# Hybrid decoder layer on one core: low parts of the second branch's weight chunks by ScalarE and an adding DMA instead of a VectorE difference

## The chip, the cores and the metric

The kernel runs on one core of a Trainium2 chip. The metric is the device time of one execution in microseconds. A core has TensorE (matmuls; PE in the profile, PEld its weight loads), VectorE (DVE), ScalarE (ACT), GpSimd (POOL) and SyncE (SP), each with its own queue of instructions that it works off in order, and 16 DMA engines that these queues feed. Here SP's queue issues the plain loads and POOL's queue issues the DMAs that add onto their destination.

## The reference

One decoder layer on 512 tokens of width 1024, in float32. What matters here is its middle part:

```python
h = rms_norm(x, mix_norm)
(fq, fk, fv, ff, dq, dk, dv, iq, ik, iw, ga, gb) = split_columns(h @ w_in)
o_a = fox_attention(fq, fk, fv, log_f).reshape(B, S, FOX_W)               # 512 columns
o_b = dsa_attention(dq, dk, dv, iq, ik, iw, rel_bias).reshape(B, S, DSA_W) # 512 columns
merged = jax.nn.sigmoid(ga) * (o_a @ w_branch_a) + jax.nn.sigmoid(gb) * (o_b @ w_branch_b)
x = x + merged @ w_out
```

Before it and behind it stands a half-step feed-forward part, `x = x + 0.5 * swiglu_ffn(x, ...)`. The change touches how the weights `w_branch_b` (512 x 1024) are got ready.

## The kernel before

**Numbers in two parts.** Every large product is done in three matmuls of a faster 32-bit format (fp32r). A float32 operand is split into a high part, which is the value rounded to fp32r, and a low part, which is the value less the high part. `mm3` (L147 to L150) multiplies high by high, high by low and low by high into the same PSUM bank. Its three lines are the three matmul lines of the profile: for a weight chunk as the first operand, L148 and L149 read the chunk's high part `wh` and L150 its low part `wl`.

**A weight chunk.** `load_w` (L127 to L145) fetches one chunk: a DMA on SP's queue brings it into a raw tile (L136), ScalarE rounds it into `wh` (L137), and then `wl` is made. Without `adding`, VectorE subtracts `wh` from the raw tile (L143). With `adding`, ScalarE writes minus `wh` into `wl` (L140), and a DMA on POOL's queue adds the raw tile onto it (L141). Raw tiles go round over three tags `ra`, `rb`, `rc` with one buffer each; `wh` and `wl` have three buffers each. So a raw tile is free for the next load when its last reader is through (the subtraction, or the adding DMA), and chunk number n + 3 can be rounded only when the matmuls of chunk n have read `wh`. Chunks 6 to 15 of the projections (the set `ADDING`, L34) already take the adding path, and so do parts of the feed-forward stages (L122, L222, L241).

**The stage of the change.** It follows the attention. In order of the program it does:

- the last gate's product (`gb7`, L1317, 24 matmuls into `ps_gb`),
- eight sigmoids of gate A (`sa`, L1313 called at L1322) with a multiplication each on VectorE (L1323),
- a loop over eight blocks d of 128 output columns (L1324 to L1336): one chunk of `w_bb` with 128 x 512 numbers, 12 matmuls of 512 columns into a bank `ps_bb`, the sigmoid of gate B, two VectorE steps into `m` (L1331, L1332), and the split of `m` into `mh` on ScalarE (L1335) and `ml` on VectorE (L1336),
- a loop over eight blocks for `w_out` (L1337 to L1344): chunks of 128 x 1024 numbers by `load_w` without `adding`, 24 matmuls each into `ps_out`, of which the last three read `mh[7]` and `ml[7]`, an addition onto x and what the next norm needs.

The chunks of `w_bb` are called bb0 to bb7 below, those of `w_out` out0 to out7. Their raw tags follow one another as ra (bb0), rb (bb1), rc (bb2), ra (bb3), and so on to rb (bb7), rc (out0).

**What sets the order.** TensorE runs in the order of the program, written out by hand (L59). The order on ScalarE, VectorE, POOL and SP in this stage is made by a planner when the kernel is built: of the instructions that its own model has ready it takes the one that stands first in the program. The instructions of `load_w` count as 30 places earlier than they stand (`high_priority`, L135), and the sigmoids are kept behind the last copy of the attention's output (L1312). On the chip each engine then keeps that order, and waits at an instruction until its inputs and its buffer are there.

Of the kernel before, what the change touches and what calls it, by code (L numbers as in the profile page):

```python
# [19 lines left out]
P = 128  # L20
# [34 lines left out]
def tile_hybrid_layer(ctx: ExitStack, tc: tile.TileContext, a: dict):  # L55
# [11 lines left out]
    def acc_tile(name):  # L67
        return psum.tile([P, T], F32, tag="acc", bufs=3, name=name)

    def tmp_tile(name):  # L70
        return tmp.tile([P, T], F32, tag="t", name=name)
# [39 lines left out]
    def raw_tile(tag):  # L111
        return wpool.tile([P, 1024], F32, tag=tag, bufs=1, name=tag)
# [14 lines left out]
    def load_w(src, n, m, raw=None, adding=False):  # L127
        f = n * m
        if raw is None:
            raw = raw_tile(next(raw_tags))  # L130
        wh = wpool.tile([P, 1088], F32R, tag="wh", name="wh")
        wl = wpool.tile([P, 1088], F32R, tag="wl", name="wl")

        wh, wl = (w[:, at:at + f] for w in (wh, wl) for at in [8 if m > P else 0])
        with tc.high_priority(offset=1 if first else 30):  # L135
            nc.sync.dma_start(raw[:, :f].rearrange("p (n m) -> p n m", n=n), src)  # L136
            S.copy(wh, raw[:, :f])  # L137
            if adding:

                S.mul(wl, wh.bitcast(F32), -1.0)  # L140
                G.dma_start(wl, raw[:, :f], accum_op=OP.add)  # L141
            else:
                V.tensor_sub(wl, raw[:, :f], wh.bitcast(F32))  # L143
        return (wh.rearrange("p (n m) -> p n m", n=n),
                wl.rearrange("p (n m) -> p n m", n=n))  # L145

    def mm3(out, lh, ll, rh, rl, start, stop, **more):  # L147
        PE.matmul(out, lh, rh, start=start, stop=False, **more)  # L148
        PE.matmul(out, lh, rl, start=False, stop=False, **more)  # L149
        PE.matmul(out, ll, rh, start=False, stop=stop, **more)  # L150

    def prep(d, gi):

        g = gains[:, gi, d:d + 1]
        if d % 2 == 0:
            for i, (part, nm) in enumerate(((xh, "xh"), (xl, "xl"))):
                t = stream(HK * i + d // 2, F32R, nm)
                part[d], part[d + 1] = t[:, :T], t[:, T:]
        S.mul(xh[d], x[d], g)
        V.scalar_tensor_tensor(xl[d], x[d], g, xh[d].bitcast(F32), op0=OP.mult, op1=OP.subtract)  # L160
# [7 lines left out]
    def add_square(d, sq=None):  # L168
        sq = sq or square(d)
        if d == 0:  # L170
            ssq[0] = sq
        else:
            V.tensor_add(ssq[0], ssq[0], sq)
# [18 lines left out]
    def fm_product(w, name, midway={}, ps=None):  # L192
        ps = acc_tile(name) if ps is None else ps
        for k in range(KD):
            mm3(ps, w[0][:, k], w[1][:, k], xh[k], xl[k], k == 0, k == KD - 1)
            if k in midway:
                midway[k]()
        return ps
# [584 lines left out]
    with (tc.tile_pool(name="mix", bufs=1) as mp, ExitStack() as att_ctx,  # L783
# [523 lines left out]
        with tc.tile_pool(name="late", bufs=1) as lp:  # L1307
            mh, ml = [], []

            def sigmoid(out, z):  # L1310

                with tc.issue_after(last_out[0].ins):  # L1312
                    S.activation(out, z, AF.Sigmoid)  # L1313

            gb[6] = lp.tile([P, T], F32, name="gb6")
            nc.sync.dma_start(gb[6], kept[:, 4])
            ps = fm_product(load_w(a["w_gb"][7], KD, P), "ps_gb")  # L1317
            gb.append(lp.tile([P, T], F32, name="gb7"))
            V.tensor_mul(gb[7], ps, rb)
            for d in range(KD):  # L1320
                sa = lp.tile([P, T], F32, tag="sa", bufs=2, name="sa")
                sigmoid(sa, ga[d])  # L1322
                V.tensor_mul(pA[d], pA[d], sa)  # L1323
            for d in range(KD):  # L1324
                wh, wl = load_w(a["w_bb"][d], 4, P)
                ps = acc_tile("ps_bb")
                for k in range(4):
                    mm3(ps, wh[:, k], wl[:, k], oB[0][k], oB[1][k], k == 0, k == 3)
                sigmoid(gb[d], gb[d])
                m = tmp_tile("m")  # L1330
                V.tensor_mul(m, ps, gb[d])  # L1331
                V.tensor_add(m, m, pA[d])  # L1332
                mh.append(lp.tile([P, T], F32R, name=f"mh{d}"))
                ml.append(lp.tile([P, T], F32R, name=f"ml{d}"))
                S.copy(mh[d], m)  # L1335
                V.tensor_sub(ml[d], m, mh[d].bitcast(F32))  # L1336
            for d in range(KD):  # L1337
                wh, wl = load_w(a["w_out"][d], KD, P)
                ps = acc_tile("ps_out")
                for k in range(KD):  # L1340
                    mm3(ps, wh[:, k], wl[:, k], mh[k], ml[k], k == 0, k == KD - 1)
                V.tensor_add(x[d], ps, x[d])
                prep(d, 2)
                add_square(d)  # L1344
# [84 lines left out]
```

## Time and profile before

| What | Value |
|---|---|
| median of 3 runs | 1073.92 us (1073.33 to 1073.96) |
| profiled execution, its own time | 1073.57 us |
| profiled execution, its span from first to last instruction | 1071.9 us |
| TensorE busy | 1056.8 us, 99% of the span |
| VectorE, ScalarE, GpSimd busy | 78%, 62%, 23% |
| granted TensorE clock, mean | 0.998 |
| the eight `w_bb` products on TensorE | from 667.4 to 690.0 us of the span |

All rows of the profile are taken from the profiled execution, in microseconds from the start of its span. A row of the timeline gives start, duration, engine, line, operation and what is written from what; a bracket at its end gives how long the engine was idle before it and what ended that wait. Rows of TensorE overlap, since matmuls are pipelined: the distance of their starts is what one costs. A row of the DMA view gives the issue, its size and the time from the issue to the landing.

### The profile page before, as it was taken

To read this page: it belongs to the slowest core of one execution; us is meant where nothing else is said; L and a number is where in the kernel's file an instruction comes from. 1 tells how busy PE (TensorE), PEld (TensorE's weight loads), DVE (VectorE), ACT (ScalarE), POOL (GpSimd) and SP (SyncE) were. 2 spreads that over 40 slices of the span, in tenths; PEclk is the share of its full clock that TensorE was granted. 3 is DMA by queue.
4 is the path that set the end of the run, shared out by engine and by line. 5 is a ranking of instruction groups with operands and counts; after the bars stand their busy time and mean duration, and the time that the engine had idled before them with its cause. 6 is when DMAs were issued, how large, how long until landed. Compare 5 with 4: busy or idle time off the path is not lost.

```text
span 1071.9 us, 19227 instructions
## 1 busy us (share of the span) xinstructions
PE 1056.8 (99%) x7330; PEld 976.2 (91%) x7330; DVE 835.2 (78%) x1374; ACT 662.4 (62%) x1098; POOL 245.1 (23%) x313
## 2 busy tenths in 40 slices
PE   9999999999999999999999999999999999999998
PEld 7889999999998889999878788788889999999998
DVE  6987888897867579976776675954977788887887
ACT  6736765765664675477766756544635764775673
POOL 1100111120000014367786563000100210111111
PEclk9999999999999999999999999999999999999999
DMA  7644764666442267733313321442653665567554
GB/s 246 148 147 115 155 161 126 141 164 167 107 110 95 75 147 190 199 96 98 90 60 99 118 89 50 144 139 76 133 157 99 137 155 163 127 160 183 128 124 129
DMA packets 55677, 140.56 MB, mean 131 GB/s; under 512 B 6424, under 2 KB 14488, under 8 KB 55584
## 3 DMA queue, kind: packets, MB, share of 16 engines
q1 hardware_dynamic: 39888, 110.22, 33.8%
q0 software_dynamic: 15552, 28.84, 15.3%
q8 instruction: 58, 0.95, 0.4%
q10 hardware_dynamic: 144, 0.26, 0.1%
q14 instruction: 35, 0.29, 0.1%
HBM read 104.94 MB, written 3.42 MB: 101 GB/s over the span
## 4 chain that ended last, share of the span: by engine, by line
PE 79%; issue 7%; DVE 5%; ACT 4%; POOL 3%; DMA 1%; SPq 0%; DVEq 0%; POOLq 0%; ACTq 0%
PE pB L149 4%; PE pB L148 4%; PE pB L150 4%; PE pA L149 3%; PE pA L148 3%; PE ps_f L148 3%; PE pA L150 3%; PE ps_f L149 3%; PE ps_f L150 3%; PE dB L148 2%; PE dB L150 2%; PE dB L149 2%; PE ps_t L148 2%; PE ps_t L150 2%; PE ps_t L149 2%
## 5 line engine op out<-in xcount | busy, mean ns | idle before, releaser
L117 ACT CAST wh<-s 128x1024 fp32r<-128x1024 f32 (+1 forms) x84 | 81.8, 974 | 62.2 <-PE pC L149 31.1
L124 DVE TENSOR_TENSOR wl<-s,wh 128x1024 fp32r<-128x1024 f32 (+1 forms) x84 | 94.5, 1125 | 27.1 <-ACT wh L117 27.1
L148 PE MATMUL ps_t<-wh,xh 128*128 128x256 f32 (+1 forms) x288 | 80.7, 280 | 0.0
L150 PE MATMUL pB<-tbh,wl 128*128 128x256 f32 x288 | 80.4, 279 | 0.0
L148 PE MATMUL pB<-tbh,wh 128*128 128x256 f32 x288 | 80.4, 279 | 0.0
L149 PE MATMUL pB<-tbl,wh 128*128 128x256 f32 x288 | 80.4, 279 | 0.0
L149 PE MATMUL ps_t<-wl,xh 128*128 128x256 f32 (+1 forms) x288 | 80.3, 279 | 0.0
L150 PE MATMUL ps_t<-wh,xl 128*128 128x256 f32 (+1 forms) x288 | 80.2, 279 | 0.0
L148 PE MATMUL ps_f<-xh,wh 128*128 128x512 f32 x152 | 61.2, 403 | 0.0
L149 PE MATMUL ps_f<-xl,wh 128*128 128x512 f32 x152 | 60.3, 397 | 0.0
L150 PE MATMUL ps_f<-xh,wl 128*128 128x512 f32 x152 | 60.2, 396 | 0.0
L148 PEld LDWEIGHTS ps_t<-wh,xh 128*128 128x128 f32 x288 | 54.3, 188 | 0.5
L149 PEld LDWEIGHTS ps_t<-wl,xh 128*128 128x128 f32 x288 | 54.3, 188 | 0.5
L150 PEld LDWEIGHTS ps_t<-wh,xl 128*128 128x128 f32 x288 | 54.3, 188 | 0.0
L148 PEld LDWEIGHTS pB<-tbh,wh 128*128 128x128 f32 x288 | 54.1, 188 | 0.0
L150 PEld LDWEIGHTS pB<-tbh,wl 128*128 128x128 f32 x288 | 54.1, 188 | 0.0
L149 PEld LDWEIGHTS pB<-tbl,wh 128*128 128x128 f32 x288 | 54.1, 188 | 0.0
L241 POOL DMA_DIRECT2D b<-gu x10 | 8.7, 865 | 198.2 <-DVE rf L441 100.7
L1140 ACT ACTIVATE p<-p,mn 128x512 f32<-128x512 f32 (+1 forms) x64 | 36.0, 562 | 28.1 <-DVE mn L1138 27.6
L1142 POOL TENSOR_SCALAR p<-p,rs 128x512 f32<-128x512 f32 (+1 forms) x64 | 38.7, 607 | 60.1 <-DVE rs L1141 58.1
L1154 DVE TENSOR_TENSOR pl<-pt,ph 128x512 fp32r<-128x512 f32 (+1 forms) x64 | 31.1, 487 | 20.6 <-ACT ph L1153 19.9
L567 POOL DMA_DIRECT2D xa<-e x16 | 19.1, 1193 | 111.6 <-ACT wh L117 87.3
(398 smaller groups left out, 4144.6 us busy)
## 6 DMA issues: line engine op xcount, KB each, us to landing
ra<-in_w_pair_dram SPq DMA_DIRECT2D x15, 512.0 KB, 4.1
rc<-in_w_pair_dram SPq DMA_DIRECT2D x15, 512.0 KB, 4.0
re<-in_w_pair_dram SPq DMA_DIRECT2D x12, 512.0 KB, 3.6
rf<-in_w_pair_dram SPq DMA_DIRECT2D x12, 512.0 KB, 3.6
rb<-in_w_pair_dram SPq DMA_DIRECT2D x12, 512.0 KB, 3.6
xa<-e POOLq DMA_DIRECT2D x18, 256.0 KB, 3.7
rd<-in_w_halves_dram SPq DMA_DIRECT2D x10, 384.0 KB, 3.8
al<-gu POOLq DMA_DIRECT2D x14, 256.0 KB, 5.3
```

Source lines behind the costliest of these rows:

```text
L117: S.copy(wh[:, :f], raw[:, :f])
L124: V.tensor_sub(wl[:, :f], raw[:, :f], wh[:, :f].bitcast(F32))
L148: PE.matmul(out, lh, rh, start=start, stop=False, **more)
L149: PE.matmul(out, lh, rl, start=False, stop=False, **more)
L150: PE.matmul(out, ll, rh, start=False, stop=stop, **more)
L241: G.dma_start(l, src, accum_op=OP.add)
L567: G.dma_start(xa[:, d:d + 2, HT:], t["e"][part], accum_op=OP.add)
L1140: S.activation(p, p, AF.Exp, bias=mn, scale=-1.0, accum_out=rs)
L1142: G.tensor_scalar(p, p, rs, 1.0, op0=OP.mult, op1=OP.mult)
L1154: V.tensor_sub(pl[:, sl], pt[:, sl], ph[:, sl].bitcast(F32))
```

## The change

The eight chunks of `w_bb` are fetched with `adding=True`. `load_w` itself is as it was; the flag chooses the branch of L140 and L141 in place of L143.

```diff
             for d in range(KD):
-                wh, wl = load_w(a["w_bb"][d], 4, P)
+                wh, wl = load_w(a["w_bb"][d], 4, P, adding=True)
                 ps = acc_tile("ps_bb")
                 for k in range(4):
                     mm3(ps, wh[:, k], wl[:, k], oB[0][k], oB[1][k], k == 0, k == 3)
```

So in each of the eight steps a VectorE subtraction of 128 x 512 numbers goes, and a ScalarE multiplication by -1 of 128 x 512 numbers and a DMA of 256 KB on POOL's queue, which adds the raw tile onto `wl`, come in its place.

## The prediction

> **What bounds the kernel now.** I read the page's busy shares first, then the stage by windows, then the timelines of TensorE, ScalarE, VectorE and SP there, then the DMA view.
>
> ```profile
> PE 1056.8 (99%) x7330; PEld 976.2 (91%) x7330; DVE 835.2 (78%) x1374; ACT 662.4 (62%) x1098; POOL 245.1 (23%) x313
> ...
> 667.20:678.00 10.80, 10.37 (x46) 8.24 (x45) 8.62 (x16) 9.90 (x19) 0.00 (x0) 1.00 0.16 49
> 678.00:690.00 12.00, 12.00 (x55) 9.94 (x54) 12.00 (x21) 6.18 (x10) 0.00 (x0) 1.00 0.63 176
> 690.00:700.00 10.00, 9.07 (x40) 7.07 (x39) 8.57 (x12) 4.47 (x6) 0.00 (x0) 1.00 0.63 234
> ```
>
> TensorE is busy 99% of the span. The window rows give the length of a stretch and then the busy time of PE, PEld, DVE, ACT and POOL, the clock, the DMA share and GB/s. In the stage of the change (667 to 690 us) VectorE is packed full from 678 on, POOL does nothing at all, and the DMA engines are quiet up to 678. Yet TensorE loses only 0.43 and 0.93 us there. Its timeline shows where:
>
> ```profile
> 672.64 0.39 PE L150 MATMUL ps_bb<-oB,wl 128*128 128x512 f32 x1
> 672.87 0.39 PE L148 MATMUL ps_bb<-oB,wh 128*128 128x512 f32 x1
> 673.10 0.39 PE L149 MATMUL ps_bb<-oB,wh 128*128 128x512 f32 x1
> 673.92 0.50 PE L150 MATMUL ps_bb<-oB,wl 128*128 128x512 f32 x1 [0.43 <-DVE wl L143]
> ...
> 689.96 0.39 PE L148 MATMUL ps_out<-mh,wh 128*128 128x512 f32 x1
> ...
> 694.04 0.39 PE L148 MATMUL ps_out<-mh,wh 128*128 128x512 f32 x1
> 695.35 0.50 PE L149 MATMUL ps_out<-ml,wh 128*128 128x512 f32 x1 [0.93 <-DVE ml L1336]
> ```
>
> A matmul costs 0.23 us (672.64 to 672.87), so a chunk of 12 takes 2.72 us. The first wait is for the low part of bb2: its third matmul starts at 673.92 where 673.33 was due, 0.59 late. The second is for the last `ml`: 695.35 where 694.27 was due, 1.08 late. These 1.7 us are all that a lighter VectorE can give back. TensorE has no other wait from 667 to 700 that VectorE causes.
>
> **What goes.** Eight subtractions of the size of this one leave VectorE (0.68 us each, 0.60 from start to start):
>
> ```profile
> 673.18 0.69 DVE L143 TENSOR_TENSOR wl<-rc,wh 128x512 fp32r<-128x512 f32 x1
> ```
>
> That is 8 x 0.60 = 4.8 us of VectorE in a stage where it is full, enough to remove the 1.08 us at the end: gain 1.1 us. The 0.59 us is counted below, since its wait changes owner.
>
> **What comes, for one chunk.** The adding path is in the trace for other chunks. Here are two of the projections (128 x 1024), and one of the feed-forward part with the 128 x 512 size, by ScalarE, POOL and SP timeline, and by the DMA view (last rows; the landings of all adds into that tile, and the median of four of them in a stretch):
>
> ```profile
> 399.61 1.05 ACT L137 CAST wh<-ra 128x1024 fp32r<-128x1024 f32 x1 [2.74 <-PE ps_t L150]
> 400.70 1.06 ACT L140 ACTIVATE wl<-wh 128x1024 fp32r<-128x1024 f32 x1
> 405.21 1.05 ACT L137 CAST wh<-rb 128x1024 fp32r<-128x1024 f32 x1 [1.30 <-PE ps_t L150]
> 406.89 1.05 ACT L140 ACTIVATE wl<-wh 128x1024 fp32r<-128x1024 f32 x1
> ...
> 402.06 0.88 POOL L141 DMA_DIRECT2D wl<-ra  x1 [1.82 <-ACT wl L140]
> ...
> 407.96 0.33 SPq L136 DMA_DIRECT2D ra<-in_w_ga_dram  x1
> ...
> 299.60 0.64 ACT L221 ACTIVATE al<-ah 128x512 fp32r<-128x512 f32 x1
> ...
> DMA to landing us min/median/max: 3.3/4.6/5.8
> ...
> al<-gu POOLq DMA_DIRECT2D x4, 256.0 KB, 4.3
> ```
>
> The multiplication follows the cast at once (400.70, the cast ends 400.66) or lets another instruction in (406.89, 0.63 after the cast's end). POOL's issue starts 0.30 after the multiplication ends (400.70 + 1.06 = 401.76, issue 402.06). The raw tile is reloaded only when the add has landed: 407.96 is 5.9 us behind the issue at 402.06. For 256 KB a landing took 3.3 to 5.8 us from the issue, and those bounds I keep. I take 4.3, since the DMA share of 0.16 from 667 to 678 is a quiet stretch. So from the start of a cast the low part takes 0.62 (cast) + 0.04 + 0.64 + 0.30 + 4.3 = 5.9 us, or 6.4 with one other ScalarE instruction (0.52 from start to start) let in; the bounds are 4.9 and 7.9. By VectorE it was there at the end of the subtraction, 673.86, which is 2.2 us behind its cast.
>
> **Which chunks that reaches.** ScalarE's order in the stage, with TensorE's change from the gate product to bb0 and POOL's last work before it:
>
> ```profile
> 653.17 0.62 ACT L137 CAST wh<-ra 128x512 fp32r<-128x512 f32 x1
> 661.72 0.62 ACT L137 CAST wh<-rb 128x512 fp32r<-128x512 f32 x1 [0.45 <-PE ps_f L149]
> 666.99 3.22 ACT L1313 ACTIVATE gb<-gb 128x512 f32<-128x512 f32 x6
> 671.68 0.61 ACT L137 CAST wh<-rc 128x512 fp32r<-128x512 f32 x1
> 672.19 0.63 ACT L1313 ACTIVATE gb<-gb 128x512 f32<-128x512 f32 x1
> 672.72 0.60 ACT L137 CAST wh<-ra 128x512 fp32r<-128x512 f32 x1
> 674.79 0.62 ACT L137 CAST wh<-rb 128x512 fp32r<-128x512 f32 x1
> ...
> 667.20 0.39 PE L150 MATMUL ps_gb<-xh,wl 128*128 128x512 f32 x1
> 667.43 0.39 PE L148 MATMUL ps_bb<-oB,wh 128*128 128x512 f32 x1
> ...
> 664.76 1.29 POOL L1174 TENSOR_TENSOR oB<-o,oB 64x512 fp32r<-64x512 f32 x1 [4.48 <-ACT oB L1173]
> ...
> rc<-in_w_bb_dram SPq DMA_DIRECT2D x2, 256.0 KB, 2.7
> rc<-in_w_out_dram SPq DMA_DIRECT2D x3, 512.0 KB, 4.1
> ```
>
> *bb0 and bb1* are rounded at 653.17 and 661.72. With 6.4 us they are whole at 659.6 and 668.1, and TensorE needs them 0.45 us into their products, at 667.9 and 670.6: hidden. Behind their two multiplications (0.52 us each) on ScalarE wait the last output copies of the attention, and behind these POOL's last step, which ends at 666.05. Its rows are read from the tenth matmul of bb0 on, at 669.5: one microsecond more costs nothing.
>
> *bb2* is rounded at 671.68, behind the sigmoids, because its `wh` buffer came free only with the gate product's last matmuls at 667.2. I leave that place as it is: the planner's condition for it doesn't change. One sigmoid (672.19) stood right behind the cast, so I take the 6.4: whole at 678.1 in place of 673.9. TensorE's queue stands behind this one matmul from 673.33: **loss 4.2 us** (2.7 with 4.9 and an unchanged place, 5.7 with 7.9).
>
> *bb3 and bb4*: their casts move back by one and two multiplications, to about 673.3 and 675.9, whole at 679.7 and 682.3. TensorE, now late, finishes bb2 at 678.1 + 10 x 0.23 = 680.4, and needs them at 680.9 and 683.6: hidden, by the delay that bb2 made.
>
> *bb5* reuses rc, which the add of bb2 holds until 678.1. Its load lands 2.7 us later, 680.9 with the issue; cast there, whole at 686.8. TensorE is through bb4 at 680.4 + 2 x 2.72 = 685.8 and needs it at 686.3: **loss 0.5 us** (0 with 3.3 landing, 2.1 with 5.8).
>
> *bb6, bb7, out0* come by the same round 2.72 us or more apart, and have 0.5 to 1.5 us to spare: rc for out0 is free at 686.8, loaded at 691.0 (4.1), and rounded and subtracted by 693.4, while TensorE, through bb7 at 694.5, wants it at 694.9. VectorE then has the last `ml` about 3.3 us behind bb7's end, 1.7 before its matmul. POOL has nothing else to do there (0.00 in the windows), and ScalarE's eight multiplications (8 x 0.52) find it half idle from 678 on (6.18 of 12.00).
>
> Without more, the sum is 4.2 + 0.5 - 1.1 = +3.6 us.
>
> **The clock.** The wait at bb2 makes TensorE idle for 4.8 us (673.33 to 678.1). The trace has one longer silence, behind the last matmul, which starts here:
>
> ```profile
> 1068.36 0.28 PE L150 MATMUL dB<-ah,wl 128*128 128x256 f32 x1
> ...
> 1070.50:1071.00 0.50, 0.00 (x0) 0.00 (x0) 0.00 (x0) 0.00 (x0) 0.00 (x0) 0.94 0.00 0
> 1071.00:1071.50 0.50, 0.00 (x0) 0.00 (x0) 0.00 (x0) 0.00 (x0) 0.00 (x0) 0.50 0.00 0
> ```
>
> The granted clock is 0.50 by 1071.0, 2.3 us behind that matmul's end. So I expect the clock halved in the wait. How long it then stays so no row shows. Bounds are nothing, and twice those 2.3 us (4.6 us at half speed lose 2.3); I take 3.4 us between them, which lose 1.7, of which 0.5 only replaces the wait of bb5: +1.2. The sum is +4.8 us. The Trainium skill, TensorE: Matmul & The Clock Gate, section "HAM oscillation — how this bites in real kernels", has the clock fall only for idle gaps over about 3.4 us; the row at the end shows it after less. By that rule the 4.8 us fall under it as well, and a wait at the lower bound (676.6, 3.3 us) wouldn't.
>
> The profiled execution's own time is 1073.57 us, 0.35 below the median. 1073.57 + 4.8 = **1078.4 us**, slower by 0.4%.
>
> **The rivals.**
>
> - *The same waits, clock untouched.* For it: the page grants full speed in every slice; but it has no such idle gap to judge by, the longest waits of TensorE being 1.1 us (row: total, times, longest). 1073.57 + 3.6 = 1077.2 us.
>
> ```profile
> PEclk9999999999999999999999999999999999999999
> ...
> PE pt L1149 <- DVE kl L804: 1.8, 3, 1.1
> ```
>
> - *The adds are slow.* With landings of 5.8 us, as the row's maximum, and more between cast and multiplication: 5.7 + 2.1 - 1.1 = +6.7, with the clock about +7.5: 1080.3 to 1081.1 us. Against it: a quiet stretch to 678; for it, 0.63 behind it.
> - *A short wait.* Landing 3.3, nothing let in, clock untouched: 2.7 - 1.1 = +1.6: 1075.2 us.
> - *No wait, the other side.* The place of bb2's cast decides it. The buffer is free at 667.2; were the planner to put the cast before the six sigmoids (666.99 to 670.2), the low part would be whole at 667.2 + 5.9 = 673.1, before 673.33. Then rc is free five microseconds sooner, bb5 is hidden too, and all 1.7 us come back: 1071.9 us. It holds while the cast starts before 667.4. For it: `load_w` counts as earlier than the sigmoids; against it: it did so before too, and still stood behind them.
>
> That the change doesn't do what it says I rule out: the same branch is in the trace at L140 and L141.
>
> **How the numbers follow.** Forecast with the clock halved 0.42; clock untouched 0.20; slow adds 0.10; a short wait 0.13; no wait 0.15. A measurement of this kernel tells about 0.2% from no change: 1071.8 to 1076.1 us. Faster than that is only the no-wait case with a little more, 0.07; within it lie the rest of that case and most of the short wait, 0.20; slower is 0.73. The range from 1073.0 to 1081.0 leaves out most of the no-wait case and the top of the slow adds.
>
> **What would show it.** Right: TensorE waits for a DMA into `wl` at the third matmul of bb2, 3 to 6 us; loads of rc 2.7 us behind the landing; the 0.93 us wait for `ml` gone; VectorE with holes from 678 to 690; a clock under 1.00 in a window behind the wait. Wrong: the cast of bb2 before 668, no DMA among what TensorE waits for, or the time gone elsewhere, in a stage that the planner has ordered anew.

## The result and the profile after

The changed kernel takes 1081.0 us (median of 6 runs, 1079.79 to 1082.74). The kernel before, beside it, takes 1073.32 us (6 runs). The ratio is 1.0073, interval 1.006 to 1.0086: 7.7 us slower, where 4.8 was predicted, and at the upper edge of the range. All times given here are medians that leave out two executions far off the others of their kernel (3706.64 us in the run with two adds, 2690.18 us in the run with eight small DMAs).

The busy shares of the page after:

```profile
PE 1057.9 (98%) x7330; PEld 977.6 (91%) x7330; DVE 832.3 (77%) x1366; ACT 667.0 (62%) x1106; POOL 251.8 (23%) x321
```

Eight instructions left VectorE, eight came to ScalarE and eight to POOL. TensorE now waits for the adds of bb2 (into `wl` from rc) and of bb7 (from rb), as its timeline after shows:

```profile
665.16 0.39 PE L148 MATMUL ps_bb<-oB,wh 128*128 128x512 f32 x1
...
670.83 0.39 PE L149 MATMUL ps_bb<-oB,wh 128*128 128x512 f32 x1
676.03 0.79 PE L150 MATMUL ps_bb<-oB,wl 128*128 128x512 f32 x1 [4.82 <-DMA wl<-rc]
676.62 0.63 PE L148 MATMUL ps_bb<-oB,wh 128*128 128x512 f32 x1
677.05 0.63 PE L149 MATMUL ps_bb<-oB,wh 128*128 128x512 f32 x1
...
679.44 0.39 PE L149 MATMUL ps_bb<-oB,wh 128*128 128x512 f32 x1
...
691.04 0.39 PE L149 MATMUL ps_bb<-oB,wh 128*128 128x512 f32 x1
692.33 0.50 PE L150 MATMUL ps_bb<-oB,wl 128*128 128x512 f32 x1 [0.90 <-DMA wl<-rb]
...
694.73 0.39 PE L148 MATMUL ps_out<-mh,wh 128*128 128x512 f32 x1
...
699.57 0.50 PE L149 MATMUL ps_out<-ml,wh 128*128 128x512 f32 x1 [0.38 <-DVE ml L1336]
```

From the first product of bb0 to the first of out0 the stage takes 694.73 - 665.16 = 29.6 us; before it was 689.96 - 667.43 = 22.5. The 7.0 us more are three items:

- bb2's third matmul starts at 676.03 where 670.83 + 0.23 = 671.06 was due: 4.97 late, 0.59 before. That is +4.4.
- Behind it eight steps (676.03 to 679.44) take 3.41 us instead of 8 x 0.23 = 1.8: +1.6. A step costs 0.43 in place of 0.23.
- bb7's third matmul starts at 692.33 where 691.27 was due: +1.06.

The slow steps are a halved clock, by windows of one microsecond (the clock is the third number from the end; the row left out has 0.50 too):

```profile
675.00:676.00 1.00, 0.00 (x0) 0.00 (x0) 1.00 (x3) 0.96 (x2) 0.00 (x0) 0.91 0.97 164
676.00:677.00 1.00, 0.97 (x2) 0.83 (x3) 0.33 (x1) 0.00 (x0) 0.75 (x1) 0.50 1.04 180
677.00:678.00 1.00, 1.00 (x4) 0.75 (x3) 0.00 (x0) 0.00 (x0) 0.10 (x1) 0.50 0.86 260
...
679.00:680.00 1.00, 1.00 (x5) 0.77 (x5) 0.00 (x0) 0.13 (x1) 0.00 (x0) 0.89 0.97 193
```

Counting the part of a microsecond that 0.91 and 0.89 stand for, the clock is at half from about 675.8 to 679.2, 3.4 us. The kernel before had such a fall too, far from this stage, and with TensorE busy in every row (0.50 also in the two rows left out):

```profile
425.00:426.00 1.00, 1.00 (x6) 0.87 (x6) 1.00 (x3) 0.73 (x2) 0.49 (x1) 0.91 0.00 0
426.00:427.00 1.00, 1.00 (x4) 0.71 (x4) 1.00 (x5) 0.00 (x0) 1.00 (x2) 0.50 0.64 139
...
429.00:430.00 1.00, 1.00 (x5) 0.77 (x5) 1.00 (x5) 0.00 (x0) 0.64 (x1) 0.88 1.03 205
```

No wait stands ahead of it, but TensorE has little to do there: from 422.40 to 424.99 it runs transposes and twenty matmuls of 8 columns each, six of them in this row of its timeline:

```profile
424.10 0.81 PE L1072 MATMUL pc<-lf,ones 128*128 128x8 f32 x6
```

The profiled execution after had no fall there. That is 1.6 of the 2.3 us by which it reached bb0 sooner (665.16 against 667.43).

How bb2's and bb7's low parts were made, from the timelines of ScalarE, POOL, SP and VectorE after:

```profile
669.10 0.61 ACT L137 CAST wh<-rc 128x512 fp32r<-128x512 f32 x1
...
670.65 1.15 ACT L1313 ACTIVATE sa<-ga 128x512 f32<-128x512 f32 x2
671.70 1.14 ACT L140 ACTIVATE wl<-wh 128x512 fp32r<-128x512 f32 x2
...
696.01 1.05 ACT L137 CAST wh<-rb 128x1024 fp32r<-128x1024 f32 x1 [2.43 <-DMA rb<-in_w_out_dram]
...
672.62 0.88 POOL L141 DMA_DIRECT2D wl<-rc  x1 [8.77 <-ACT wl L140]
...
686.93 0.86 POOL L141 DMA_DIRECT2D wl<-rb  x1 [1.85 <-ACT wl L140]
...
685.34 0.33 SPq L136 DMA_DIRECT2D rc<-in_w_out_dram  x1
687.76 0.33 SPq L136 DMA_DIRECT2D ra<-in_w_out_dram  x1
...
697.09 1.23 DVE L143 TENSOR_TENSOR wl<-rb,wh 128x1024 fp32r<-128x1024 f32 x1 [1.05 <-ACT wh L137]
698.23 0.68 DVE L1332 TENSOR_TENSOR m<-m,pA 128x512 f32<-128x512 f32 x1
```

And the landings of the DMAs into `wl` after, from 672 to 693 us:

```profile
DMA to landing us min/median/max: 3.3/3.8/5.4
```

In bb2 the multiplication came 2.6 us behind the cast, with four instructions let in (a gate B sigmoid, bb3's cast and two gate A sigmoids); the add then took only 676.03 - 672.62 = 3.4 us. bb7's add took 692.33 - 686.93 = 5.4, the maximum, while SP had two 512 KB loads under way (rc and ra for out0 and out1, issued at 685.34 and 687.76). The row at 696.01 shows what followed. The raw tile rb stayed held, so out2's load started late, its cast at 696.01 waited 2.43 us, and VectorE's subtraction for it (697.09), queued ahead of the last `m` (698.23), kept the last `ml` 0.5 us late (1.08 before): only 0.5 of the 1.1 us came back.

Where both kernels' matmuls are the same, their distance to before can be followed to the end: +4.77 at out0, +4.26 behind the wait for `ml`, 4.2 from 750 to 975, 4.75 from 1040, 5.87 at the last one (1068.36 before, 1074.23 after). So 1.6 us came where nothing was changed. The 0.55 us of them are a stretch from about 980 to 1040 that runs 1% slower; the same two POOL issues lie 31.22 us apart before (1001.68, 1032.90) and 31.51 after (1006.05, 1037.56). For the rest, POOL's last rows before:

```profile
1050.46 1.20 POOL L555 DMA_DIRECT2D xa<-e  x1 [15.07 <-ACT wh L117]
1052.55 1.19 POOL L555 DMA_DIRECT2D xa<-e  x1 [0.89 <-DVE xa L552]
1053.28 1.38 POOL L511 DMA_DIRECT2D re<-rc  x1
```

And after, with a row of ScalarE and one of TensorE behind them:

```profile
1056.02 1.20 POOL L555 DMA_DIRECT2D xa<-e  x1 [15.93 <-issue]
1058.63 1.19 POOL L555 DMA_DIRECT2D xa<-e  x1 [1.41 <-DVE s L502]
1059.37 1.37 POOL L511 DMA_DIRECT2D re<-rc  x1
...
1065.46 0.83 ACT L117 CAST wh<-re 128x768 fp32r<-128x768 f32 x1 [4.11 <-DMA re<-rc]
...
1066.84 0.39 PE L148 MATMUL dB<-ta,wh 128*128 128x256 f32 x1 [0.54 <-ACT dC L587]
```

VectorE's rows there are 4.97 us behind those of before:

```profile
1051.57 0.68 DVE L552 SCALAR_TENSOR_TENSOR xa<-dC,xa 128x512 f32<-128x512 f32 x1
...
1056.54 0.69 DVE L552 SCALAR_TENSOR_TENSOR xa<-dC,xa 128x512 f32<-128x512 f32 x1
```

Against them the issues at 1056.02 and 1058.63 come 0.6 and 1.1 us late, the add into re with them, its cast on ScalarE waits 4.11 us (2.46 before), and TensorE passes the place 1.1 us later.

The profiled spans close: -2.3 + 7.0 - 0.5 - 0.1 + 0.55 + 1.1 = +5.75, against 1077.7 - 1071.9 = 5.8. The own times differ by 1079.79 - 1073.57 = 6.2. The medians differ by 7.7, about one clock fall more. The mean granted clocks on record fit that: 0.998 in the profiled execution after, which is one fall (0.5 x 3.4 / 1077.7 = 0.0016), and 0.995 to 0.997 in four of the other five. Where those falls lay, no trace tells.

### The profile page after: what moved, and what is told of

Its sections match the earlier page's. It is cut to its first block, busy times and chain, and to the rows that moved or that the text cites. A ratio compares the mean times of both kernels' runs of the same rounds, so it can differ in the third digit from the quotient of the medians.

```text
span 1077.7 us, 19247 instructions
## 1 busy us (share of the span) xinstructions
PE 1057.9 (98%) x7330; PEld 977.6 (91%) x7330; DVE 832.3 (77%) x1366; ACT 667.0 (62%) x1106; POOL 251.8 (23%) x321
## 5 line engine op out<-in xcount | busy, mean ns | idle before, releaser
L1140 ACT ACTIVATE p<-p,mn 128x512 f32<-128x512 f32 (+1 forms) x64 | 35.9, 562 | 28.5 <-DVE mn L1138 27.9
```

The lines of the kernel that those rows point to most:

```text
L1140: S.activation(p, p, AF.Exp, bias=mn, scale=-1.0, accum_out=rs)
```

## Experiments

### The parts alone: bb0 and bb1, and bb2

```diff
-wh, wl = load_w(a["w_bb"][d], 4, P, adding=True)
+wh, wl = load_w(a["w_bb"][d], 4, P, adding=d < 2)     # first run
+wh, wl = load_w(a["w_bb"][d], 4, P, adding=d == 2)    # second run
```

> Only bb0 and bb1 take the adding path. Theory (the adds are too late where the cast is late, elsewhere they are hidden): both are whole microseconds before TensorE wants them, so the time is that of before, 1073.3 us within 0.7. Rival (each add costs its share, by its traffic or its issue): 2 of 8 of the 7.7 us, 1075.2 us. Rival (the planner's new order costs it, wherever it is): any time, without a DMA among what TensorE waits for.

Measured: 1072.52 us, 0.9989 of before (0.9978 to 0.9999). The stage took 21.8 us and no product waited for an add. Adds that have time cost nothing.

> Only bb2 takes the adding path. Theory: TensorE waits 4 to 5 us at its third matmul, the clock is halved for 3.4 us behind it, and most of the loss is there: 1078.5 to 1080 us; the wait of 0.9 us at bb7 is gone, since bb7 goes by VectorE. Rival (each add costs its share): one of eight, 1074.3 us.

Measured: 1078.08 us, 1.0041 (1.0026 to 1.0056), a little under the theory's numbers:

```profile
676.90 0.79 PE L150 MATMUL ps_bb<-oB,wl 128*128 128x512 f32 x1 [4.66 <-DMA wl<-rc]
```

With this one chunk the stage takes 29.5 us, nearly the change's 29.6; the clock is at half for about 6.8 us behind this wait. It makes somewhat more than half of the 7.7 us.

### Is the clock's fall the wait's doing?

Twenty small matmuls into a spare bank between bb2's second and third matmul keep TensorE at work in the wait.

```diff
+if (d, k) == (2, 0):
+    PE.matmul(ps, wh[:, 0], oB[0][0], start=True, stop=False)
+    PE.matmul(ps, wh[:, 0], oB[1][0], start=False, stop=False)
+    spin = psum.tile([P, T], F32, tag="pt", bufs=2, name="spin")
+    for _ in range(20):
+        PE.matmul(spin[:, 0:P], ones, ones, start=True, stop=True)
+    PE.matmul(ps, wl[:, 0], oB[0][0], start=False, stop=False)
+    continue
```

> As the changed kernel, with 20 small matmuls of ones into a spare bank between the second and the third matmul of bb2, which fill TensorE's wait and are read by nobody. Theory (the clock is halved because TensorE stands idle): full speed behind the wait, which is worth 1.6 us there; up to 0.5 us of it can come back as a wait at bb5. 1079.0 to 1080.0 us, that is 1.0 to 1.6 below the changed kernel. Rival (the clock falls by itself, whatever TensorE does): the same 1081.0 us, or more by what the small matmuls overrun.

Measured: 1080.63 us, 1.0069 (1.005 to 1.0087). The clock stood at 1.00 in every window from 660 to the last matmul, so the fall does hang on TensorE's idleness in the wait. The time was a miss: hardly better than the change. The stage still took 28.5 us, 1.1 less than the change's, a wait of 0.9 for bb7's add stayed, and so did a rest of bb2's:

```profile
677.57 0.50 PE L1334 MATMUL ps_bb<-oB,wl 128*128 128x512 f32 x1 [0.55 <-DMA wl<-rc]
```

### bb2's low part sooner

First the negative copy is made from the raw tile (rounded to the same value), so that it need not wait for the cast; then bb2 gets tiles of its own, so that cast and copy need not wait for the gate product's buffer; then bb2 to bb4 do.

```diff
-S.mul(wl, wh.bitcast(F32), -1.0)
+S.mul(wl, raw[:, :f] if adding == 2 else wh.bitcast(F32), -1.0)
-wh, wl = load_w(a["w_bb"][d], 4, P, adding=True)
+wh, wl = load_w(a["w_bb"][d], 4, P, adding=2)                                              # first run
+wh, wl = load_w(a["w_bb"][d], 4, P, adding=2, own=(lp, 9 - d) if d == 2 else None)          # second run
+wh, wl = load_w(a["w_bb"][d], 4, P, adding=2, own=(lp, 9 - d) if 1 < d < 5 else None)       # third run
```

> As the changed kernel, but ScalarE's negative copy of the eight chunks is taken from the raw tile (rounded to the same format, so the same numbers), not from the high part, and so stands right behind the cast in ScalarE's order. Theory: the add of bb2 is issued 2.1 us sooner, TensorE's wait there falls from 4.8 to about 3 us, and the time to about 1079 us (1078.3 to 1079.7). Rival (each add costs its share): 1081.0 us as before.

Measured: 1080.14 us, 1.0061 (1.0041 to 1.0081), a miss. The wait shrank as expected, but the shorter wait still brought a fall of the clock, and a longer one:

```profile
675.07 0.80 PE L150 MATMUL ps_bb<-oB,wl 128*128 128x512 f32 x1 [3.27 <-DMA wl<-rc]
```

The clock was at half from 673.8 to 680.6, 6.8 us, and gave back most of what the earlier copy had won. bb7's add landed in 3.7 us here and nothing waited for it, though the same two loads were under way.

> As with the negative copy from the raw tile, and bb2's high and low parts lie in tiles of their own (those of mh7 and ml7, not yet in use), so its cast needn't wait for the gate product's buffers and stands before the sigmoids. All eight adds stay. Theory (the place of the cast decides, by way of the buffer): no wait at bb2, short ones at bb3 and bb6 of 0.2 to 0.9 us, no fall of the clock: 1072.0 to 1074.0 us. Rival (eight adds cost 7.7 us by their traffic or issue): 1079 us or more.

Measured: 1077.62 us, 1.0037 (1.0024 to 1.0051), 3.6 us above the theory's range. bb2 no longer waits and the clock holds in the stage, but bb3 and bb7 wait:

```profile
678.16 0.50 PE L150 MATMUL ps_bb<-oB,wl 128*128 128x512 f32 x1 [0.94 <-DMA wl<-ra]
691.45 0.50 PE L150 MATMUL ps_bb<-oB,wl 128*128 128x512 f32 x1 [1.63 <-DMA wl<-rb]
```

> The same with tiles of their own for bb2, bb3 and bb4. Theory: every low part is whole before TensorE wants it, and VectorE has room, so all 1.7 us of the kernel before come back: 1071.0 to 1072.5 us. Rival (some cost of the adds that stays, by traffic or issue): not under 1073.3 us.

Measured: 1075.83 us, 1.0024 (1.0016 to 1.0033): 5 us under the change with all eight adds in place, and still over before. TensorE's and ScalarE's timelines:

```profile
687.41 0.50 PE L150 MATMUL ps_bb<-oB,wl 128*128 128x512 f32 x1 [1.01 <-DMA wl<-rb]
...
681.35 0.62 ACT L137 CAST wh<-rb 128x512 fp32r<-128x512 f32 x1 [3.84 <-DMA rb<-in_w_bb_dram]
```

bb7's cast waits for its load, because bb4's add held the same raw tile: the load is issued at 675.97, when that add has landed, and the cast starts 5.4 us later. A raw tile goes round through load, cast, copy and add in three chunks, and 3 x 2.72 = 8.2 us are short for that. Three more waits were not expected: 0.30 us for bb6's add, which took 7.1 us, 0.69 for VectorE, and 1.34 for the last `ml`. The own tiles themselves, with all lows on VectorE:

> The kernel before (low parts by VectorE), with the same tiles of their own for bb2, bb3 and bb4. It tells what the tiles alone bring. Theory: the wait at bb2 goes (0.59 us), the wait for the last ml of 1.08 us stays, because VectorE has as much to do as before: 1072.5 to 1073.3 us. Were the tiles all that matters, it would be as fast as the kernel with adds and own tiles.

Measured: 1073.54 us, 1.0003 (0.9994 to 1.0011). The tiles are worth nothing measurable by themselves, so they do not make the 5 us; what they save with the adds is waits.

### VectorE's load the other way: gate A's products on GpSimd

```diff
-V.tensor_mul(pA[d], pA[d], sa)
+G.tensor_mul(pA[d], pA[d], sa)
```

This is the kernel before, with POOL idle from 667 to 690 put to use.

> The kernel before, with the eight multiplications of gate A (pA by sa) on POOL, which has nothing else to do in the stage, instead of VectorE. It takes the same 4.8 us from VectorE as the change does, without a DMA. Theory (VectorE's load is worth 1.7 us at most, and any way to lighten it without making a low part late gets part of it): 1072.0 to 1073.0 us. Rival (VectorE's load in the stage costs nothing): 1073.3 us.

Measured: 1076.76 us, 1.003 (1.002 to 1.0041), a miss with the wrong sign. POOL's and VectorE's timelines:

```profile
670.99 8.09 POOL L1323 TENSOR_TENSOR pA<-pA,sa 128x512 f32<-128x512 f32 x5 [2.61 <-ACT sa L1313]
...
672.75 1.79 DVE L143 TENSOR_TENSOR wl<-ra,wh 128x512 fp32r<-128x512 f32 x1
674.46 0.68 DVE L1331 TENSOR_TENSOR m<-ps_bb,gb 128x512 f32<-128x512 f32 x1
...
683.29 0.68 DVE L143 TENSOR_TENSOR wl<-ra,wh 128x512 fp32r<-128x512 f32 x1
```

While POOL multiplies (671 to 679.1, 1.6 us each), VectorE's subtractions take 1.8 us in place of 0.68; the step that reads PSUM (674.46) keeps its 0.68, and at 683.29, with POOL done, so does the subtraction. TensorE then waits 1.61 us for bb4's low part and 1.79 for the last `ml` (0.93 before), and behind this second wait the clock is at half for 3.4 us, from 698.2 to 701.7.

### Which of the other adds are late?

```diff
+wh, wl = load_w(a["w_bb"][d], 4, P, adding=d < 2 or d > 4)       # five adds
+wh, wl = load_w(a["w_bb"][d], 4, P, adding=d in (0, 1, 5, 6))    # four adds
```

> Adds for chunks 0, 1, 5, 6 and 7 alone; chunks 2 to 4 keep VectorE's difference, so the 4.4 us wait of chunk 2 and its clock fall cannot come. Theory A (one late add at the start of the round makes the rest): the stage takes 22 to 22.5 us, no wait for an add over 0.3 us, time 1072.5 to 1073.5. Theory B (an add takes longer to come back, 3.4 to 5.4 us behind a cast, a negative copy and an issue, than the eight products of 2.72 us leave a raw tile, so the later adds wait by themselves): waits of 0.5 to 1.6 us each on wl of chunk 5, 6 or 7, stage 23.5 to 25 us, time 1074.5 to 1076. Last stage (first product of the last dA to first of the last dB): 13.4 us by both, if its lengthening needs more than 16384 packets on GpSimd's DMA queue (here 16272).

Measured: 1074.84 us, 1.0018 (1.0009 to 1.0027): between the theories, and neither's mechanism. TensorE's timeline:

```profile
680.19 0.50 PE L150 MATMUL ps_bb<-oB,wl 128*128 128x512 f32 x1 [0.41 <-DMA wl<-rc]
687.85 0.50 PE L150 MATMUL ps_bb<-oB,wl 128*128 128x512 f32 x1 [1.93 <-DMA wl<-rb]
```

The window behind the second wait, and the landings of the DMAs into `wl` from 674 to 692:

```profile
688.00:692.00 4.00, 4.00 (x13) 3.10 (x14) 2.91 (x5) 2.14 (x3) 0.00 (x0) 0.66 0.75 269
```

```profile
DMA to landing us min/median/max: 3.9/4.2/6.8
```

bb7's add was issued at 681.04 and needed until 687.84, 6.8 us, between loads of 512 KB issued at 680.20 and 682.31; bb5's and bb6's came in time or 0.4 late. After 1.9 us of waiting the clock fell again. Taking bb7's add away as well:

> Adds for chunks 0, 1, 5 and 6 alone. With five adds chunk 7's took 6.8 us from issue to landing beside two loads of the output weights, and its product waited 1.9 us. If that collision is what kept five adds above before: waits of at most 0.4 us for an add (chunk 5's, as there), time 1072.7 to 1073.5, at most 0.3 over before. If a second round of adds is too slow for any chunk: chunk 6 now waits 1 us or more, time 1074 to 1075.

Measured: 1072.04 us beside 1072.74 for before, 0.9994 (0.9984 to 1.0003). No product waits for an add. So what remained was bb7's add, and no second round as such. That the loads for the output projection slow this add is argued, not shown: every add over 5 us had loads under way beside it, but with the copy made at once bb7's landed in 3.7 us beside the same two loads. This and the first run (bb0 and bb1 alone) are the only placings of the adds that do no harm. The two adds of the first run together with own tiles for bb2 to bb4, whose lows stay on VectorE (`adding=d < 2, own=(lp, 9 - d) if 1 < d < 5 else None`):

> Before, with adds for chunks 0 and 1 alone and tiles of their own for chunks 2 to 4, whose lows stay on VectorE: the two edits that cost nothing alone, together. If PE's products bound the stage: 21.8 us for it (eight times 2.72), as each edit alone gave, time 1072.3 to 1073.3, no faster than with the first edit alone.

Measured: 1072.28 us, 0.9996 (0.9987 to 1.0005), stage 689.35 - 667.59 = 21.8 us, which is eight times 2.72: there is no more to be had in this stage than 22.5 - 21.8 = 0.7 us.

### The microsecond at the end

DMAs from GpSimd that nobody reads, added to the kernel before: eight and twenty small ones, then eight and twenty of 256 KB.

```diff
+for i in range(1):                        # or 3 if d < 4 else 2
+    G.dma_start(lp.tile([P, 8], F32, name=f"dum{d}{i}"), gains[:, 0, :8])                  # in the w_bb loop
+    G.dma_start(lp.tile([P, T], F32, tag="sa", bufs=2, name="idle"), gb[d])                # in the w_out loop
```

> The kernel before, with eight DMAs of 128 x 8 elements from GpSimd into tiles that nobody reads, in the second branch's loop: 16704 packets on GpSimd's DMA queue, as with eight adds, and hardly any bytes. Theory C (the lengthening of the last stage hangs on the count of descriptors that GpSimd has issued, 1024 on each of its 16 rings, which the third last DMA or the one behind it passes): the last stage is 14.2 to 14.5 us, POOL's second last xa<-e comes 1.2 us or more behind its operand, time 1.0 us over before. Rival D (it hangs on the adds' bytes or on the phase in which the branch ends): 13.4 us there and the time of before.

Measured: 1075.72 us, 1.003 (1.002 to 1.004). Its profile is of the execution of 2690 us, so its stages can't be read; the next run suggests a second cause for its time.

> As the run with eight idle DMAs, but twenty of them: 18432 packets, so that the 16384th falls about eleven DMAs before the end, among the rows of line 241 some 50 us earlier. Theory C: the last stage is back at 13.4 us, and one or two of POOL's issues near that earlier place come about 1 us late; time within 0.5 us of before, or up to 1 us over it if a product waits there. Rival (any larger number of GpSimd's DMAs makes the last stage longer): 14.2 us or more there, time 1 us or more over before.

Measured: 1076.24 us, 1.0035 (1.0021 to 1.0049). The small DMAs stood ahead of POOL's last step of the attention and made TensorE wait 2.2 us for `oB`; the last stage was not longer than before. They were 32 packets each instead of the 144 of an add, so the threshold that I had supposed was not passed.

> The kernel before, with eight DMAs of 128 x 512 elements (no add) from GpSimd into scratch tiles that nobody reads, in the output projection's loop, where POOL is idle: 16704 packets on GpSimd's DMA queue, as with the eight adds, the eight small ones having been 256 packets only. Theory C (the late issues near the end hang on how many descriptors GpSimd has issued by then): the stretch from PE's products at 1053 to those at 1063 of before grows by 0.9 to 1.1 us, the second last xa<-e is 1 us late behind its operand, time 1.0 over before. Rival D (it hangs on the adds or on the second branch's timing): no lateness there and the time of before.

Measured: 1073.44 us, 1.0012 (1.0002 to 1.0021). POOL's last rows:

```profile
1048.55 1.20 POOL L555 DMA_DIRECT2D xa<-e  x1 [15.07 <-ACT wh L117]
1051.74 1.19 POOL L555 DMA_DIRECT2D xa<-e  x1 [1.99 <-DVE s L502]
```

And one of TensorE's waits from 1040 us on:

```profile
PE dB L148 <- ACT dC L587: 0.9, 1, 0.9
```

The second issue is 1.1 us late, and TensorE loses 1.45 us in this profile: the microsecond, without a single add. In the four other runs with all eight adds TensorE loses 0.9 to 1.1 us at the same place; in the readable profiles of all other runs it loses nothing there.

> As the run before this one, but twenty such DMAs: 18432 packets. Theory C with one threshold near 16384: the late issues move some ten DMAs earlier, among the rows of line 241 or 567 around 980 to 1035, and the last three are on time; the end grows by up to 1 us only where a product waits for a late one. A rival of C (each DMA more makes the last three later): 1.1 us or more in the last stage. Rival D: the time of before.

Measured: 1073.06 us, 1.0004 (0.9994 to 1.0013). Here the first of the three is 0.7 us late and the second on time again, and nothing waits:

```profile
1051.82 1.20 POOL L555 DMA_DIRECT2D xa<-e  x1 [15.79 <-issue]
1053.24 1.19 POOL L555 DMA_DIRECT2D xa<-e  x1 [0.22 <-issue]
```

So the loss goes with how many DMAs GpSimd has issued before: none with up to four more, a late second row that nobody waits for with five, a microsecond with eight, none with twenty. A late issue moves from place to place, and costs time where a product waits. My threshold fell: these DMAs were 80 packets each, and the loss came with 16192 packets on GpSimd's queue in all, but not with as many in the run with twenty small ones, nor with 16272 (five adds). What makes an issue late stays open.

## Why the prediction was right and wrong

The forecast was 2.9 us short. Two steps of it failed most: that bb6, bb7 and out0 have time to spare (bb7 lost 1.06), and that POOL's issues cost nothing because it has nothing else to do there (1.1 behind the stage). The gain at the last `ml` was 0.6 too large.

- **Direction and main mechanism: right.** bb2's add is late because its cast stays behind the sigmoids, and this chunk alone costs 0.41%, about 4.4 us. bb0 and bb1 cost nothing, as said.
- **bb2, 4.2 us: right in size, partly by luck, since its errors cancel.** The prediction let one ScalarE instruction in between cast and multiplication; four came (2.6 us). It took 4.3 for the landing; 3.4 was measured, and the cast came 0.3 sooner behind bb0's start (669.10 - 665.16 against 671.68 - 667.43). Result 4.4.
- **The clock, length right by luck, claims wrong.** The 3.4 us, a choice between two bounds, were measured to the tenth, with 1.6 lost for the 1.7 assumed; the same wait with bb2 alone brought 6.8. And the statement that no row shows how long a fall lasts was wrong: the 425 to 430 windows of before show one. The page's clock line, in tenths of 40 slices, hides it; the mean of 0.998 does not. The fall replaced no wait either: the 0.5 set off against bb5 wasn't there.
- **bb5, and "bb6, bb7, out0 ... have 0.5 to 1.5 us to spare": these steps failed.** bb5 was to lose 0.5 and lost nothing, since its add landed in 3.3 us. bb7, which the sum had hidden, lost 1.06, since its add took 5.4 us beside the loads for the output projection. The prediction kept 5.8 as the upper bound of a landing, in the rival with slow adds, but put it at bb2 and bb5, in a quiet stretch, where it wasn't. So the measured time lies within that rival's 1080.3 to 1081.1 us, but not by its way.
- **The gain of 1.1 at the last `ml`: mis-sized.** 0.5 came back. The step overlooked that bb7's raw tile feeds out2, whose subtraction stands ahead of the last `m` on VectorE.
- **Not in the sum at all: 1.6 us behind the stage; the step that POOL's issues are free failed.** The 1.1 in the last stage belongs to the change, by way of GpSimd's number of DMAs; why an issue comes late stays open. The prediction counted POOL's eight issues as free because POOL was idle in the stage, and didn't follow POOL's queue to its end. The 0.55 at 1% slower pace came in ten of the other fourteen readable profiles, there or some 88 us earlier, that of gate A's products on GpSimd, without a new add, among them, and in four not (own tiles for bb2 alone, own tiles without adds, own tiles with two adds, four adds); it can't be shown to be the change's.

By its own terms: 4.2 + 0.5 - 1.1 + 1.2 = 4.8 became 4.4 + 0 + 1.06 - 0.5 + 1.6 + 1.1 = 7.7. The equality with the medians' difference is closer than its parts, since the clock falls differ from one execution to another by 1.6 us each.

The Trainium skill, TensorE: Matmul & The Clock Gate, section "HAM oscillation — how this bites in real kernels", gives an idle gap over about 3.4 us as the condition. The runs agree with a length of 3.4 us or twice that for each fall, but not with the condition: the clock fell after waits of 3.27 us (the copy made at once), 1.93 (five adds) and 1.79 (gate A on GpSimd), and in before at 425.8 with no wait at all. It held after the 1.63 of the run with own tiles and the 2.21 of the run with twenty small DMAs.

The traces hold more on this. Within a profile all changes of the clock lie whole multiples of 3.413 us apart: in before 1070.94 - 429.24 = 641.70 = 188 x 3.413, after 1078.59 - 679.23 = 399.36 = 117 x 3.413. Cut into stretches at these points, the waits fall in order. The clock fell behind a stretch in which TensorE was idle for 1.71 us or more in sum (1.71 at the kernel's end with five adds, 1.79 with gate A on GpSimd, 1.93 with five adds, 2.01 with the copy at once, all 3.41 after). It held behind 1.78 us or less (1.60 with bb2's own tiles; of the 2.21 us with twenty small DMAs, 1.78 lay in one stretch). So the limit lies at 1.7 to 1.8 us, half a stretch. The fall lasted a second stretch where the first one still held 0.93 us of the wait (bb2 alone) or 1.26 (the copy at once), and only one where it held 0.22 (after). The fall at 425.8 fits roughly if the tiny matmuls count as little work: it came in the eight profiles where one stretch took in 2.3 to 2.6 us of them, and not in the seven where none took in more than 2.4. No run was made to test this. If it holds, the same wait can cost a fall in one execution and none in the next, since the points lie elsewhere in each.

## What to carry to other kernels

Replacing an engine's short step by a DMA lengthens the way from the cast to the operand from about 2 us to 5 to 8, so it belongs only where a chunk is rounded that much ahead of its product; place by place, the first, second, sixth and seventh chunk could carry it here and the third could not. A raw tile that such a DMA reads is held until it lands, which took longest here while the next stage's loads ran: check the round of buffers to its end, not only the first late operand. Look at the clock by microseconds around each wait of more than about 1.7 us, since it can cost itself and 1.6 us or more on top. Follow the queue of the engine that takes over the work to the end of the kernel, not only through the stage.

## What the runs showed of the hardware that I had not expected

- The clock halves for 3.4 us or twice that (675.8 to 679.2; 673.8 to 680.6), also after a wait of only 1.79 us, and not by the wait's length alone: 4.82 us of waiting brought one length, 3.27 brought two, and 2.21 none. Its changes lie on a raster of 3.413 us, and idleness of half a stretch of it was enough.
- An add of 256 KB within SBUF landed 3.3 to 7.1 us after its issue; those over 5 us had loads under way beside them.
- VectorE's subtractions on SBUF took 1.8 us in place of 0.68 while GpSimd multiplied; its step that reads PSUM kept its 0.68.
- GpSimd's issues came 0.6 to 1.1 us late at some DMAs, at a place that moved with the number of DMAs it had issued before.
